# Two low-rank projections of layer 0 moved in beside the modulation, by quarters of their rows

## Chip, core and metric

The kernel runs on one core of a Trainium2 chip. The metric is the device time of one execution in microseconds; lower is better.

## What is computed

Two layers of a trunk in which four token mixers run in parallel on one normalised, modulated input. Layer 0 works on 256 latent and 256 context tokens of 2048 channels:

```python
mod_x = silu(c) @ w_mod[l] + b_mod[l]        # and the same from c_ctx for the context
shift, scale, gate = split(mod_x, 3)
hx = rmsnorm(x, pre_g[l]) * (1 + scale) + shift
px = split_proj(hx @ w_in[l])                # kv 320, cq 512, zA, uB, ... 512 each, gates 8192 columns
q  = rmsnorm(px.cq, q_norm_g) @ w_uq         # low rank, then 4 heads
kv = rmsnorm(px.ckv, kv_norm_g) @ w_ukv
ya = attention(q, kv) * silu(px.zA)
yb = fourier_mix(px.uB) * silu(px.zB)        # yc, yd: a short convolution and a spatial gate
out = (sum over g of sigmoid(gate_g) * (y_g @ w_branch[g])) @ w_out
x  = x + gate * rmsnorm(out, post_g)
```

All of it is in float32.

## The kernel before

Every large product is made from float32 operands that are split into a high and a low half. A chunk of weights is 256 rows by 512 columns (512 KB, one transfer into a `raw` tile of five); ScalarE casts its two halves of 128 rows to `wh` (L236), VectorE subtracts to get `wl` (L239), and TensorE makes three matmuls for each of four output tiles and each 128 rows: high times high, low times high, high times low (L263 to L265 where the features are the rows of the result, L267 to L269 where the tokens are). A projection from 2048 channels is eight such chunks, 192 matmuls into four banks of `acc`; `acc` has five banks, `mis` (transposes, scores) three.

Layer 0 has to make its own modulation first. `mod_products(l, part, j)` makes one part (scale, part 1, or shift, part 0) of 512 columns: eight transfers of 512 KB from `w_mod`, each followed by two narrow matmuls (L315) against the silu of `c` and `c_ctx`, 32 columns wide and in one of four quarters of the array; then a copy on ScalarE (L318), four transposes (L321), and small steps on VectorE (L323, L324, L299, L301). With both parts of a unit of four blocks of 128 channels there, `to_modulate` makes the eight pieces of the input for these channels: ScalarE applies scale and shift (L392), VectorE splits (L208, L209). The rows of `x` and `ctx` are read in four tiles of 1 MB, normalised (L378 on ScalarE, the chain to L387 on VectorE) and transposed (L398) beside the first unit.

The modulation stage runs over four units of four blocks. cq of layer 0 is accumulated in four banks from the first unit to the last: after the first part of unit j, the two chunks of cq for the channels of unit j-1 follow (`first_steps`), and the last two after the stage. Then kv (eight chunks of 320 columns) with the norm of cq beside it, the query and key products with the norm of kv beside them, then zA and uB with the attention of the layer beside both, and the gates.

Work that is to lie beside a projection stands in two queues: `near`, which moves one step at every chunk (`tick`), and `far`, the modulation of later parts on VectorE (`mod_sums`, L338), which moves 0.65 steps a chunk. The framework orders the instructions of each engine at build time from the order of the code; each engine works its list in order and waits on semaphores.

Of the kernel before, what the change touches and what calls it, by code (L numbers as in the profile page):

```python
# [25 lines left out]
P = 128  # L26
# [3 lines left out]
W = 512  # L30
# [6 lines left out]
FIRST_AT = (0, 7)  # L37
# [8 lines left out]
def in_groups():  # L46

    out = {n: (OFF[n], 320 if n == "kv" else W) for n in ORDER}
    for g in range(4):
        for d in range(4):  # L50
            out[f"g{g}{d}"] = (GATES + g * D + d * W, W)
    return out
# [18 lines left out]
def layouts(inp):  # L71
# [6 lines left out]
    for l in range(L):  # L78
        a[f"wi{l}"] = chunked(inp["w_in"][l], gin)
        a[f"wm{l}"] = chunked(inp["w_mod"][l], [slice(i * W, (i + 1) * W) for i in range(12)])  # L80
# [64 lines left out]
def backbone(ctx: ExitStack, tc: tile.TileContext, a, out):  # L145
# [82 lines left out]
    def chunk(src, off, n, on_act=True):  # L228
# [3 lines left out]
        for k in range(KC):  # L232
            h = pw.tile([P, W], F32R, tag="wh", name="wh", bufs=NH)[:, :n]
            l = pw.tile([P, W], F32R, tag="wl", name="wl", bufs=NL)[:, :n]
            if on_act:
                nc.scalar.copy(h, raw[:, k, :])  # L236
            else:
                ve.tensor_copy(h, raw[:, k, :])
# [11 lines left out]
    def projecting(banks, src, off, nk, n, mode, ah, al, on_act=True):  # L250
# [4 lines left out]
        for kc in range(nk // KC):  # L255
            wh, wl = chunk(src, off + kc * KC * P * n, n, on_act)
            for j, kk in order(len(banks), kc == nk // KC - 1):
# [14 lines left out]
    def project(src, off, nk, n, mode, ah, al, size):  # L272

        banks = [bank([P, size]) for _ in range(n // P)] if mode == "f" else [bank([P, n]) for _ in range(size)]
        for _ in projecting(banks, src, off, nk, n, mode, ah, al):
            tick()
        return banks
# [14 lines left out]
    def mod_done(l, part, j, streams, vals):  # L292

        c = slice(j * 4, (j + 1) * 4)
# [10 lines left out]
    def mod_products(l, part, j):  # L305


        b = bank([P, W])
        i = part * 4 + j
        for kc in range(KD // KC):  # L310
            raw = raw_chunk(a[f"wm{l}"], (i * (KD // KC) + kc) * KC * P * W)
            for kk in range(KC):
                k = kc * KC + kk
                q = (k % 4) * 32
                mm(b[q:q + 32, :], cvz[:, k, :], raw[:, kk, :], start=k < 4, stop=k >= KD - 4, tile_position=(0, q))  # L315
            yield
        r = small([P, W])
        nc.scalar.copy(r, b)  # L318
        tr = bank2([P, 4, P])
        for q in range(4):  # L320
            nc.tensor.transpose(tr[:, q, :], r[:, q * P:(q + 1) * P], ident)  # L321
        c2 = pv.tile([P, 4, 2], F32, tag="c2", name="c2", bufs=2)
        ve.reduce_sum(c2, tr.rearrange("p b (q m) -> p b m q", q=4)[:, :, 0:2, :], axis=AX.X)  # L323
        mod_done(l, part, j, (0, 1), lambda v, m: ve.tensor_copy(m, c2[:, :, v]))  # L324

    def mod_sums(l, part, j, streams):
# [27 lines left out]
        mod_done(l, part, j, streams, lambda v, m: ve.reduce_sum(m, own[:, v], axis=AX.X))  # L354
# [51 lines left out]
    first_mod = mod_products(0, 1, 0)  # L406
    for _ in range(3):
        next(first_mod)

# [8 lines left out]
    xs = [big("m", [P, 4, 512]) for _ in range(4)]  # L418

    def rows_in():  # L420
        for v, src in enumerate((a["x"], a["ctx"])):
            tiles = []
            for i in range(2):
                x = big("y" if v + i == 2 else "t", [P, D])
                nc.sync.dma_start(x, src[i * P:(i + 1) * P, :])
                scaled_rows(x)
                tiles.append(x)
                yield
# [36 lines left out]

    h0 = Input(0)
    rows = rows_in()
    cq0 = [bank([P, W]) for _ in range(4)]
    first = projecting(cq0, a["wi0"], offs["cq"], KD, W, "t", *h0.acts("t", W))

    def first_steps(j):
        for _ in range(2):
            next(first)

    def to_modulate(j):
        for k in range(4 * j, 4 * j + 4):
            for v in range(2):
                c = slice(v * NS, (v + 1) * NS)
                modulated(0, k, v, xs[j][:, k % 4, c], [h0.part(k, i, v * NS, (v + 1) * NS) for i in range(2)])
                yield  # L480

    pending = iter(())
    for j in range(4):
        for part in (1, 0):
            g = mod_products(0, part, j) if (part, j) != (1, 0) else first_mod
            for n, _ in enumerate(g):
                if j == 0:
                    next(rows, None)
                next(pending, None)
                if j and (part, n) == FIRST_AT:  # L490
# [5 lines left out]
        pending = to_modulate(j)  # L496
# [4 lines left out]
    first_steps(3)  # L501
# [5 lines left out]
    def layer(l, hx, cq):  # L507
# [7 lines left out]
        def hin(name, mode, tiles=nt):  # L515
            n = 320 if name == "kv" else W
            return project(a[f"wi{l}"], offs[name], KD, n, mode, *hx.acts(mode, T), T if mode == "f" else tiles)
# [8 lines left out]
        def low_rank(bs, n, sizes):  # L526

            raw = big("t", [P, 4, 512])
            ssq = tiny(4)
            for i, b in enumerate(bs):  # L530
                nc.scalar.copy(raw[:, i, :sizes], b[:, :sizes])
                sum_squares(ssq[:, i:i + 1], raw[:, i, :n])
            return raw, ssq, len(bs), n
# [28 lines left out]
        if cq is None:  # L562
            cq = hin("cq", "t")
        cq = low_rank(cq, W, W)
        near.append(normed(cq, qg, qh, ql))
# [3 lines left out]
        kv = hin("kv", "t", 4)  # L569
        drain(near)  # L570
        kv = low_rank(kv, 256, 320)
        raw = kv[0]
        kvs = big("m", [P, 4, 512], F32R)
        kh, kl = kvs[:, 0:2, :], kvs[:, 2:4, :]
        if not last:
            qn = big("t", [P, 4, 512])
        near.append(normed(kv, kg, kh, kl))
# [534 lines left out]
```

## Time and profile before

| | us |
|---|---|
| median of 3 runs | 2648.08 (2646.14 to 2648.66) |
| profiled execution | 2649.58 |
| its span, first to last instruction | 2647.8 |
| TensorE busy | 2597.5 |
| VectorE busy | 1568.4 |
| ScalarE busy | 1032.4 |

The profiled execution is a little longer than its span, since something lies around the first and last instruction. Busy times are those of the engines by themselves; they overlap. A busy TensorE can still run below its full clock, which the granted clock of a stretch tells.

### The profile page before, as it was taken

The page shows a single profiled execution, that of the slowest core. Times are in us where ns is not written, and L with a number is a line of the kernel's source. Part 1 is how long each engine was busy: PE and PEld are TensorE (multiplying, and loading weights), DVE is VectorE, ACT ScalarE, POOL GpSimd, SP SyncE. Part 2 cuts the span into 40 slices and gives each one's busy share as a digit, 9 for nine tenths or more (in the row PEclk, how much of TensorE's full clock was granted, in tenths as well). Part 3 has the DMA queues.
Part 4 walks back from the last instruction along what each step waited for, and adds up shares of the span by engine and source line. Part 5 has one row for each costly group of instructions (what it writes and reads, how often), then busy time and mean ns, then how long its engine had stood idle before and what let it go on. Part 6 is the DMA issues. An engine that isn't in the chain of part 4 may idle for free.

```text
span 2647.8 us, 32990 instructions
## 1 busy us (share of the span) xinstructions
PE 2597.5 (98%) x11739; PEld 2098.5 (79%) x11739; DVE 1568.4 (59%) x2964; ACT 1032.4 (39%) x1881; POOL 11.5 (0%) x25
## 2 busy tenths in 40 slices
PE   6899999999999999999999999999999999999998
PEld 2387788888888888888888888889788888888886
DVE  4277465666666567555563336776555555656666
ACT  3244333222222222222222235565655444545555
POOL 0000000000000000000000000000000000000000
PEclk8999999999999999999999999999999999999999
DMA  8754243444435444445453326754445555566566
GB/s 324 289 181 144 88 135 132 148 159 151 151 136 167 153 151 155 153 141 178 144 177 102 97 97 213 254 167 141 139 151 175 191 193 195 186 208 200 187 219 206
DMA packets 125493, 448.61 MB, mean 169 GB/s; under 512 B 14112, under 2 KB 19408, under 8 KB 123408
## 3 DMA queue, kind: packets, MB, share of 16 engines
q1 hardware_dynamic: 123088, 433.11, 48.6%
q0 software_dynamic: 2240, 13.40, 1.4%
q8 instruction: 92, 1.51, 0.2%
q14 instruction: 73, 0.60, 0.1%
HBM read 442.23 MB, written 4.22 MB: 169 GB/s over the span
## 4 chain that ended last, share of the span: by engine, by line
PE 95%; DMA 2%; DVE 2%; ACT 0%; issue 0%; SPq 0%; DVEq 0%; ACTq 0%
PE acc L263 16%; PE acc L265 16%; PE acc L264 16%; PE acc L269 14%; PE acc L267 14%; PE acc L268 14%; DMA raw<-in_wm 2%; PE acc L315 1%; PE mis L398 1%; PE mis L660 1%; PE mis L661 1%; DVE m L1020 0%; DVE wl L239 0%; PE mis L644 0%; PE mis L857 0%
## 5 line engine op out<-in xcount | busy, mean ns | idle before, releaser
L239 DVE TENSOR_TENSOR wl<-raw,wh 128x512 fp32r<-128x512 f32 (+1 forms) x1256 | 848.0, 682 | 741.0 <-PE acc L265 345.4
L236 ACT CAST wh<-raw 128x512 fp32r<-128x512 f32 (+1 forms) x1256 | 769.6, 617 | 1323.9 <-PE acc L264 814.6
L267 PE MATMUL acc<-wh,hh 128*128 128x512 f32 (+1 forms) x1568 | 611.5, 390 | 0.0
L263 PE MATMUL acc<-hh,wh 128*128 128x512 f32 x1536 | 602.9, 393 | 0.2 <-DVE m L780 0.2
L269 PE MATMUL acc<-wl,hh 128*128 128x512 f32 (+1 forms) x1568 | 601.4, 384 | 1.4 <-DVE wl L239 1.3
L268 PE MATMUL acc<-wh,hl 128*128 128x512 f32 (+1 forms) x1568 | 601.3, 383 | 0.0
L265 PE MATMUL acc<-hh,wl 128*128 128x512 f32 x1536 | 598.3, 390 | 0.0
L264 PE MATMUL acc<-hl,wh 128*128 128x512 f32 x1536 | 598.0, 389 | 0.0
L338 DVE SCALAR_TENSOR_TENSOR ma<-raw,cv,ma 128x512 f32<-128x512 f32 x420 | 298.6, 747 | 141.3 <-DMA raw<-in_wm 139.8
L269 PEld LDWEIGHTS acc<-wl,hh 128*128 128x128 f32 x1568 | 294.3, 188 | 61.5 <-DVE wl L239 4.7
L267 PEld LDWEIGHTS acc<-wh,hh 128*128 128x128 f32 x1568 | 294.8, 188 | 58.2 <-issue 2.9
L268 PEld LDWEIGHTS acc<-wh,hl 128*128 128x128 f32 x1568 | 294.9, 188 | 57.9 <-issue 2.9
L263 PEld LDWEIGHTS acc<-hh,wh 128*128 128x128 f32 x1536 | 288.4, 188 | 61.1 <-DVE m L780 0.8
L265 PEld LDWEIGHTS acc<-hh,wl 128*128 128x128 f32 x1536 | 288.3, 188 | 60.5
L264 PEld LDWEIGHTS acc<-hl,wh 128*128 128x128 f32 x1536 | 288.4, 188 | 60.0 <-issue 0.7
L263 PE MATMUL acc<-y,wh 128*128 128x512 f32 x256 | 101.4, 396 | 0.0
L264 PE MATMUL acc<-y,wh 128*128 128x512 f32 x256 | 100.9, 394 | 0.0
L265 PE MATMUL acc<-y,wl 128*128 128x512 f32 x256 | 100.9, 394 | 0.0
L315 PE MATMUL acc<-raw,g 128*32 128x512 f32 x256 | 64.5, 707 | 24.6 <-DMA raw<-in_wm 24.6
L315 PEld LDWEIGHTS acc<-raw,g 128*32 128x32 f32 x256 | 9.9, 117 | 65.6 <-DMA raw<-in_wm 50.5
L265 PEld LDWEIGHTS acc<-y,wl 128*128 128x128 f32 x256 | 47.9, 187 | 11.8
L263 PEld LDWEIGHTS acc<-y,wh 128*128 128x128 f32 x256 | 47.9, 187 | 11.7
(220 smaller groups left out, 1497.6 us busy)
## 6 DMA issues: line engine op xcount, KB each, us to landing
raw<-in_wi SPq DMA_DIRECT2D x432, 512.0 KB, 3.5
raw<-in_wm SPq DMA_DIRECT2D x192, 512.0 KB, 4.3
raw<-in_wo SPq DMA_DIRECT2D x104, 512.0 KB, 4.2
raw<-in_wb SPq DMA_DIRECT2D x64, 512.0 KB, 4.1
raw<-in_wi SPq DMA_DIRECT2D x16, 320.0 KB, 3.3
t<-row POOLq DMA_DIRECT2D x3, 1024.0 KB, 6.8
t<-in_x SPq DMA_DIRECT2D x2, 1024.0 KB, 9.7
raw<-in_wq SPq DMA_DIRECT2D x4, 512.0 KB, 4.3
```

Of the source, the lines that this page charges most:

```text
L236: nc.scalar.copy(h, raw[:, k, :])
L239: ve.tensor_tensor(l, raw[:, k, :], h.bitcast(F32), ALU.subtract)
L263: mm(b, wh[kk][:, c], xh, start=first, stop=False)
L264: mm(b, wh[kk][:, c], xl, start=False, stop=False)
L265: mm(b, wl[kk][:, c], xh, start=False, stop=last)
L267: mm(b, xh, wh[kk], start=first, stop=False)
L268: mm(b, xl, wh[kk], start=False, stop=False)
L269: mm(b, xh, wl[kk], start=False, stop=last)
L315: mm(b[q:q + 32, :], cvz[:, k, :], raw[:, kk, :], start=k < 4, stop=k >= KD - 4, tile_position=(0, q))
L338: ve.scalar_tensor_tensor(s, raw[:, kk, :], cv[:, k, v:v + 1], s, ALU.mult, ALU.add)
L398: nc.tensor.transpose(dst[:, i * P:(i + 1) * P], x[:, k * P:(k + 1) * P], ident)
L660: mm(s, qn[:, h, c], kn[:, h, k0:512], start=True, stop=False)
```

## The change

Five edits, all in layer 0.

1. The row tiles of `x` and `ctx` are issued to the queue before any weight of the modulation.
2. The modulation's units are now (first block, blocks) = (0,2), (2,2), (4,4), (8,4), (12,4): the first unit of four is cut in two. A unit of four reads alternately a 1 MB tile (in `y`) and two 512 KB tiles, four matmuls to a step.
3. cq and kv are made by quarters of their rows (four blocks of 128 channels): a quarter accumulates in four banks, and its sums go to SBUF (`parked`), copied by ScalarE for the first quarter and added by VectorE for the others. Sixteen pieces of one chunk each, in the order cq, cq, kv, kv for each quarter; `BESIDE` places 0, 1, 3, 4, 3 of them in the five units, the other five come after the last.
4. uB follows kv directly, with the norms of cq and kv as its `near` work.
5. zA has the attention beside it alone, with a `near` step after every half chunk (`fine`).

```diff
-FIRST_AT = (0, 7)
+UNITS = ((0, 2), (2, 2), (4, 4), (8, 4), (12, 4))
...
-    def tick():
+    def tick(whole=True):
         step(near)
-        pace[1] += pace[0]
+        pace[1] += pace[0] if whole else 0.0
...
-    def projecting(banks, src, off, nk, n, mode, ah, al, on_act=True):
+    def projecting(banks, src, off, nk, n, mode, ah, al, fine=False):
...
+            for at, (j, kk) in enumerate(order(len(banks), kc == nk // KC - 1)):
+                if fine and at == len(banks):
+                    yield
...
+    def mod_products(l, part, k0, nk):
+        n = nk * P
+        b = bank([P, n])
+        for s in range(KD // 4):
+            off = moff[l][part * D + k0 * P] + s * 4 * P * n
+            if n < W:
+                raw = pw.tile([P, KC, W], F32, tag="raw", name="raw", bufs=NR).rearrange("p k n -> p (k n)")
+            elif s % 2 == 0:
+                raw = big("y", [P, 2048])
+            else:
+                raw = None
...
+            for i in range(4):
+                mm(b[i * 32:(i + 1) * 32, :], cvz[:, s * 4 + i, :], rows[i], start=s == 0, stop=s == KD // 4 - 1,
+                   tile_position=(0, i * 32))
+            yield
...
+    for v, src in enumerate((a["x"], a["ctx"])):
+        for i in range(2):
+            rows_of[v, i] = x = big("y" if v + i == 2 else "t", [P, D])
+            nc.sync.dma_start(x, src[i * P:(i + 1) * P, :])
...
+    def quarter(name, j):
+        n = 320 if name == "kv" else W
+        if j == 0:
+            parked[name] = big("t", [P, 4, W])
+        banks = [bank([P, n]) for _ in range(4)]
+        ah, al = h0.acts("t", W)
+        for kc in (2 * j, 2 * j + 1):
+            wh, wl = chunk(a["wi0"], offs[name] + kc * KC * P * n, n)
+            for i, kk in order(4, kc % 2):
+                k = kc * KC + kk
+                mm(banks[i], ah(k, i), wh[kk], start=k == 4 * j, stop=False)
+                mm(banks[i], al(k, i), wh[kk], start=False, stop=False)
+                mm(banks[i], ah(k, i), wl[kk], start=False, stop=k == 4 * j + 3)
+            if kc % 2:
+                for i, b in enumerate(banks):
+                    s = parked[name][:, i, :n]
+                    if j == 0:
+                        nc.scalar.copy(s, b)
+                    else:
+                        ve.tensor_tensor(s, s, b, ALU.add)
+            yield
...
+    products = in_turn(*[quarter(name, j) for j in range(4) for name in ("cq", "kv")])
+    BESIDE = (0, 1, 3, 4, 3)
     pending = iter(())
+    for u, (k0, nk) in enumerate(UNITS):
+        at = [1 + 7 * i // max(BESIDE[u], 1) for i in range(BESIDE[u])]
+        for n, _ in enumerate(in_turn(mod_products(0, 1, k0, nk), mod_products(0, 0, k0, nk))):
...
+            if n in at:
+                if n == at[0]:
                     for _ in pending:
                         pass
-                    first_steps(j - 1)
+                next(products)
...
+        pending = to_modulate(k0, nk)
...
-    first_steps(3)
+    for _ in products:
+        pass
...
+        near.append(normed(kv, kg, kh, kl))
         if not last:
+            u = big("t", [P, 4, 512])
+            fourier_in()
+            drain(near)
             qn = big("t", [P, 4, 512])
...
-            za = silu("zA")
-            u = big("t", [P, 4, 512])
-            fourier_in()
+            za = silu("zA", fine=True)
             drain(near)
```

Lines move: the narrow matmul L315 is L337 in the changed file, its copy and transposes L341 and L344, the cast `wh` L245, the modulation L392 is L415, the wide matmuls of cq and kv are L502 to L504.

The queue's list (SP) at the start of the program, before the change; `t` and `y` hold rows, `raw` weights:

```order
3 L225 DMA raw<-in_wm 128x1024 x3
4 L412 DMA cst<-in_const 128x260
5 L225 DMA raw<-in_wm 128x1024
6 L425 DMA t<-in_x 128x2048
7 L225 DMA raw<-in_wm 128x1024
8 L425 DMA t<-in_x 128x2048
9 L225 DMA raw<-in_wm 128x1024 x5
10 L425 DMA t<-in_ctx 128x2048
11 L225 DMA raw<-in_wm 128x1024
12 L425 DMA y<-in_ctx 128x2048
```

and of the changed kernel:

```order
3 L431 DMA cst<-in_const 128x260
4 L442 DMA t<-in_x 128x2048 x2
5 L442 DMA t<-in_ctx 128x2048
6 L442 DMA y<-in_ctx 128x2048
7 L330 DMA raw<-in_wm 128x2x512 x10
8 L235 DMA raw<-in_wi 128x1024
```

Four transfers of weights stood ahead of the first row tile, and eleven ahead of the last; now none does.

ScalarE's list before, from the second unit to the third; L392 is the modulation of the input, L236 the casts of cq's weights:

```order
15 L392 ACTIVATE s<-m,mod_78 128x256 x8
16 L318 COPY s<-acc 128x512 x2
17 L236 CAST wh<-raw 128x512 x2
18 L392 ACTIVATE s<-m,mod_78 128x256 x2
19 L236 CAST wh<-raw 128x512 x2
20 L392 ACTIVATE s<-m,mod_78 128x256 x6
21 L318 COPY s<-acc 128x512 x2
```

and of the changed kernel, from the third unit to the fifth (L415 modulates, L245 casts):

```order
26 L341 COPY s<-acc 128x512
27 L415 ACTIVATE s<-m,mod_78 128x256 x8
28 L245 CAST wh<-raw 128x512 x4
29 L245 CAST wh<-raw 128x320 x2
30 L341 COPY s<-acc 128x512
31 L245 CAST wh<-raw 128x320 x2
32 L341 COPY s<-acc 128x512
33 L415 ACTIVATE s<-m,mod_78 128x256 x8
34 L245 CAST wh<-raw 128x512 x4
```

The casts stood ahead of the pieces of modulation of their own unit; they now stand behind all eight of them.

TensorE's list before, around the first piece of cq:

```order
46 L315 MATMUL acc<-raw,g 32x512 x12
47 L321 MATMUL mis<-cst,s 128x128 x4
48 L315 MATMUL acc<-raw,g 32x512 x16
49 L321 MATMUL mis<-cst,s 128x128 x4
50 L267 MATMUL acc<-wh,hh 128x512
51 L268 MATMUL acc<-wh,hl 128x512
```

and of the changed kernel at the end of the third unit, where the second quarter of cq begins:

```order
149 L337 MATMUL acc<-y,g 32x512 x4
150 L337 MATMUL acc<-raw,g 32x512 x4
151 L344 MATMUL mis<-cst,s 128x128 x4
152 L337 MATMUL acc<-y,g 32x512 x4
153 L337 MATMUL acc<-raw,g 32x512 x4
154 L502 MATMUL acc<-wh,hh 128x512
155 L503 MATMUL acc<-wh,hl 128x512
```

Between the last transposes of a unit and the first product that needs it there stood a whole part (16 narrow matmuls and its transposes); there now stand eight narrow matmuls.

## Rows read from the trace of the kernel before

**Rows 1.** the page: busy time, share of the span and instructions of each engine

```profile
PE 2597.5 (98%) x11739; PEld 2098.5 (79%) x11739; DVE 1568.4 (59%) x2964; ACT 1032.4 (39%) x1881; POOL 11.5 (0%) x25
```

**Rows 2.** waits of PE in the whole span: total us, times, longest

```profile
PE acc L315 <- DMA raw<-in_wm: 24.6, 27, 5.8
PE mis L398 <- DVE t L387: 6.2, 2, 5.1
```

**Rows 3.** stretches: length, PE, PEld, DVE, ACT, POOL busy, granted clock, DMA, GB/s

```profile
0.00:69.17 69.17, 47.56 (x209) 13.96 (x209) 29.79 (x123) 24.08 (x64) 0.20 (x4) 0.90 0.86 327
...
80.87:102.18 21.31, 14.61 (x74) 3.07 (x73) 0.83 (x7) 1.74 (x4) 0.00 (x0) 1.00 0.91 342
...
113.88:138.38 24.50, 17.34 (x74) 4.08 (x73) 0.83 (x7) 2.00 (x4) 0.00 (x0) 0.77 0.83 312
...
10.00:20.00 10.00, 5.33 (x17) 0.96 (x15) 4.32 (x21) 5.12 (x16) 0.00 (x0) 0.71 1.02 413
```

**Rows 4.** PE in order of time, modulation: start, us, operation, idle before

```profile
80.87 2.77 PE L315 MATMUL acc<-raw,g 128*32 128x512 f32 x20
85.53 1.05 PE L315 MATMUL acc<-raw,g 128*32 128x512 f32 x4 [1.89 <-DMA raw<-in_wm]
```

**Rows 5.** PE in order of time, the cq and kv products

```profile
71.24 0.39 PE L267 MATMUL acc<-wh,hh 128*128 128x512 f32 x1
...
80.55 0.39 PE L269 MATMUL acc<-wl,hh 128*128 128x512 f32 x1
...
161.32 0.30 PE L267 MATMUL acc<-wh,hh 128*128 128x320 f32 x1
...
168.21 0.31 PE L269 MATMUL acc<-wl,hh 128*128 128x320 f32 x1
...
191.37 0.31 PE L268 MATMUL acc<-wh,hl 128*128 128x320 f32 x1
```

**Rows 6.** ACT, then DVE in order of time: the four row tiles

```profile
12.42 0.63 ACT L378 ACTIVATE s<-t 128x512 f32<-128x512 f32 x1 [9.74 <-DMA t<-in_x]
...
15.01 0.16 DVE L385 TENSOR_REDUCE n<-n 128x1 f32<-128x4 f32 x1 [11.89 <-ACT s L378]
...
22.34 1.29 DVE L387 TENSOR_SCALAR t<-t,n 128x2048 f32<-128x2048 f32 x1
...
39.80 1.29 DVE L387 TENSOR_SCALAR y<-y,n 128x2048 f32<-128x2048 f32 x1
...
49.38 0.42 DVE L436 COPY m<-mis 128x256 f32<-128x256 f32 x1 [1.15 <-PE mis L398]
```

**Rows 7.** PE, ACT, DVE in order of time: a unit's end and its modulation

```profile
68.65 0.66 PE L321 MATMUL mis<-cst,s 128*128 128x128 f32 x4 [0.73 <-ACT s L318]
...
49.59 0.66 PE L321 MATMUL mis<-cst,s 128*128 128x128 f32 x4
...
50.97 4.04 ACT L392 ACTIVATE s<-m,mod 128x256 f32<-128x256 f32 x8 [1.00 <-DVE mod L299]
...
55.49 0.75 DVE L209 TENSOR_TENSOR hl<-s,hh 128x256 fp32r<-128x256 f32 x2
```

**Rows 8.** stretches of 2 us; columns as in rows 3

```profile
32.00:34.00 2.00, 0.00 (x0) 0.00 (x0) 1.25 (x8) 2.00 (x7) 0.00 (x0) 1.00 0.94 309
34.00:36.00 2.00, 0.00 (x0) 0.00 (x0) 1.72 (x9) 0.89 (x4) 0.00 (x0) 0.69 0.90 334
...
40.00:42.00 2.00, 2.00 (x6) 0.56 (x5) 1.31 (x2) 0.12 (x1) 0.00 (x0) 0.60 0.64 190
42.00:44.00 2.00, 1.97 (x10) 0.86 (x9) 0.95 (x3) 0.85 (x3) 0.00 (x0) 1.00 0.87 344
```

**Rows 9.** groups by shape to 420 us: busy, mean ns, idle before, releaser

```profile
L338 DVE SCALAR_TENSOR_TENSOR ma<-raw,cv,ma 128x512 f32<-128x512 f32 x93 | 66.3, 745 | 22.4 <-DMA raw<-in_wm 22.4
L663 DVE TENSOR_REDUCE n<-mis 128x1 f32<-128x512 f32 x8 | 5.5, 690 | 7.6 <-PE mis L661 7.5
...
L666 ACT ACTIVATE s<-mis,n 128x512 f32<-128x512 f32 x8 | 5.5, 689 | 16.9 <-DVE n L664 16.9
```

More of the change, by code (lines that the diff above doesn't have):

```diff
@@ L51, in in_groups, with mod_groups @@
             out[f"g{g}{d}"] = (GATES + g * D + d * W, W)
+    return out
+def mod_groups(l):
+    out = []
+    for part in range(3):
+        units = UNITS if l == 0 and part < 2 else [(4 * j, 4) for j in range(4)]
+        out += [(part * D + k * P, n * P) for k, n in units]
     return out
@@ L303, in mod_done @@
                 ve.tensor_tensor(m, m, vecs[l][:, 86:102][:, c], ALU.mult)
[L305 to L315, printed above, removed]
+    moff = {l: {c: D * c for c, _ in mod_groups(l)} for l in range(L)}
@@ L466, in backbone @@
     h0 = Input(0)
[L467 to L476, printed above, removed]
+    parked = {"cq": None, "kv": None}
+    def quarter(name, j):
[16 more added lines that the diff above has]
+                        nc.scalar.copy(s, b)
+                    else:
+                        ve.tensor_tensor(s, s, b, ALU.add)
+            yield
@@ L477, in to_modulate, with in_turn @@
+    def to_modulate(k0, nk):
+        for k in range(k0, k0 + nk):
             for v in range(2):
                 c = slice(v * NS, (v + 1) * NS)
-                modulated(0, k, v, xs[j][:, k % 4, c], [h0.part(k, i, v * NS, (v + 1) * NS) for i in range(2)])
+                modulated(0, k, v, xs[k // 4][:, k % 4, c], [h0.part(k, i, v * NS, (v + 1) * NS) for i in range(2)])
                 yield
-    pending = iter(())
[L483 to L487, printed above, removed]
+    def in_turn(*gens):
+        for g in gens:
+            yield from g
@@ L523, in cols, with low_rank @@
             return lambda k, j: h[:, k, j * P:(j + 1) * P], lambda k, j: l_[:, k, j * P:(j + 1) * P]
-        def low_rank(bs, n, sizes):
-            raw = big("t", [P, 4, 512])
+        def low_rank(name, n, sizes, tiles):
             ssq = tiny(4)
-            for i, b in enumerate(bs):
-                nc.scalar.copy(raw[:, i, :sizes], b[:, :sizes])
+            if last:
+                bs = hin(name, "t", tiles)
+                raw = big("t", [P, 4, 512])
+            else:
+                raw = parked[name]
+            for i in range(tiles):
+                if last:
+                    nc.scalar.copy(raw[:, i, :sizes], bs[i][:, :sizes])
                 sum_squares(ssq[:, i:i + 1], raw[:, i, :n])
-            return raw, ssq, len(bs), n
+            return raw, ssq, tiles, n
         def normed(rows, g, dh, dl):
@@ L568, in layer @@
             drain(near)
-        kv = hin("kv", "t", 4)
-        drain(near)
-        kv = low_rank(kv, 256, 320)
+        kv = low_rank("kv", 256, 320, 4)
+        if last:
+            drain(near)
         raw = kv[0]
@@ L683, in silu @@
                 yh, yl = halves()
-            for f, b in enumerate(hin(name, "f")):
+            for f, b in enumerate(hin(name, "f", fine=fine)):
                 s = small([P, 512])[:, :T]
```

81 lines of the change are left out of this document (39 added, 42 removed).

## The prediction

> **What bounds the kernel now.** I read the page first: TensorE is busy for 98% of the span [rows 1], so a change can win only where TensorE waits, runs slowly, or does a thing twice. Then the waits of TensorE: nearly all of the idle time stands at two places, in front of the modulation's products (for weights) and in front of the transposes of the input rows (for VectorE) [rows 2]. Both lie in the first 138 us. The stretches of that stage [rows 3] show the pattern: between two pieces of cq, 21.3 and 24.5 us in which TensorE is busy for 14.6 and 17.3 us, while the transfers run at 342 and 312 GB/s. After that stage TensorE works without a gap, kv included. So what the change is worth is read from the start of the program to the end of kv, at 191.5 us (the last start of [rows 5] and the 0.15 us that one takes); what follows (the query and key products, attention, zA, uB) is the same TensorE work in both kernels, 44 us of uB included, which only changes places with kv.
>
> The reference point is therefore this: before, cq and kv are done at 191.5 us. In the changed kernel the same state is the start of uB. The four groups of transposes of cq's norm, 0.45 us each (0.66 with the drain of the last in it [rows 7]), stand ahead of that point before and behind it now, 1.8 us. The gain is 191.5 - 1.8 - X, where X is the time at which uB starts.
>
> **What the change adds up to, step by step.**
>
> *The input rows.* All four row tiles are now issued ahead of any weight, after 0.2 MB of constants. Before, the first tile was there at 12.4 us [rows 6], behind some 2 MB of weights and shared with more of them; at 413 GB/s [rows 3] those 2 MB are 5 us, so I take 8 us (bounds 6.5 and 10). ScalarE's sums take 2.6 us (12.42 to 15.01), then VectorE needs 8.6 us for two tiles (15.01 to 22.34 + 1.29), 4.3 each and 17.2 for four; on it also lie eight copies of the first half, 0.42 us each, 3.4. The second half's transposes and copies took from 41.1 to 49.8 us, 8.7 [rows 6]. That is 8 + 2.6 + 17.2 + 3.4 + 8.7 = 39.9, where the trace of before has 49.8. The modulation of the first two blocks of 128 columns lies beside this; its end needs 2.6 us (small copies, one cast of 0.6, one subtraction of 0.7, a first modulated piece). The first product starts at **42.5 us** (bounds 40, and 52.4 if the rows come no sooner).
>
> *The products.* cq is 192 matmuls: 42 of them from 71.24 to 80.55, 0.227 us apart; kv is 192, 48 from 161.32 to 168.21, 0.147 apart [rows 5]. 43.6 + 28.2 = **71.8 us**, unchanged in number.
>
> *The modulation's products.* One transfer of 512 KB gives two matmuls, each recorded twice: 20 records in 2.77 us are five transfers, 0.55 us each when the weights are there; a lone one takes 1.05 [rows 4]. Of the 64, ten lie in the first 42.5 us, 54 x 0.55 = 29.7, and seven groups of four transposes, 3.1: **32.8 us**. That the weights are there: by the end of the last unit the queue has moved 42.7 MB (64 x 0.524, 4.2 of rows, six cq and five kv chunks); at the 327 GB/s of the first stretch [rows 3] that is 131 us, and my sum has that end at 143. The 1 MB tiles help here, but transfers are not the term that sets X.
>
> *The new wait, at the hand-over of a unit.* Before, cq's piece j came a whole part (eight transfers) after the modulation of its rows; the cast of its weights stood ahead of the pieces of modulation on ScalarE. Now the product of a unit stands three steps behind the end of that unit, and the order of ScalarE shows eight pieces of modulation, and only then the casts that the product waits for. Price [rows 7]: 0.73 us copy, 1.38 from the transposes to the first piece (49.59 to 50.97), 4.04 for the eight, 0.62 for a cast: 6.8, with latencies 6.9 us. VectorE ends its last split at 56.24 and then has a subtraction of 0.7, 7.3 us after the transposes began, which the first four matmuls cover. Meanwhile TensorE has its transposes (0.45) and four transfers' products (2.2): 4.25 us are left, at two hand-overs (k 4 to 7, k 8 to 11). The unit of two blocks has half the pieces, 2.3. After the last unit nothing is left to fill with: kv's third quarter is ready in its data, but its casts stand behind the same eight pieces, 6.45. Sum **17.3 us**. If the pieces hid as before, 0; if VectorE ends it instead of ScalarE, 2 us more.
>
> *The clock.* [...] Four hand-overs with idle stretches of 2.3 to 6.4 us: **8.6 us** (bounds 0, and 22 from the rival below). [...]
>
> *Smaller ones.* Sums now leave the banks after each quarter: seven of eight quarters end in four VectorE adds or ScalarE copies beside the next piece; I take 0.3 us for each of ten starts of a piece, **3.0** (bounds 0 and 6).
>
> X = 42.5 + 71.8 + 32.8 + 17.3 + 8.6 + 3.0 = 176.0, and the gain 191.5 - 1.8 - 176.0 = 13.7 us.
>
> *uB beside the norms* costs nothing: the norms' 24 transposes wait on VectorE while uB's 192 matmuls, 44 us, run; uB itself needs only the modulated input. If that cover failed, it is the one wait of 1.1 us that cq's norm has before.
>
> *zA beside attention.* The 16 steps of attention now stand 12 matmuls (2.7 us) apart instead of 24. A step's chain is maximum 0.69, exponential 0.69 [rows 9], some 0.5 of small ones: 1.9 us, and the far queue's four accumulations of 0.745 can stand ahead on VectorE, 3.0: 4.9. A score bank comes round after 2.7 plus 0.5 to 2 us of attention's own matmuls. I take 0; worst 1.5 us at five steps, 7.5.
>
> The profiled execution took 2649.6 us around its span of 2647.8; less 13.7 it is 2635.9. The median of the runs shown is 1.5 us lower, so I forecast **2634 us**.
>
> **The rivals.**
> *A. The clock holds, and the rows come early.* For it: the stretch 80.87 to 102.18 is idle for a third and yet at full clock [rows 3]. Against: the clock at 34 to 42 us [rows 8]. The gain is 13.7 + 8.6 + 2.5 = 24.8: 2623 us.
> [...]
> *C. Slower: attention becomes the bound.* Place: the score matmuls, waiting for a bank that the exponential of the step before still reads. It decides from 13.7 / 16 = 0.86 us a step; with 1.5 at every step it is 24 us, 10 slower: 2658. For it: the 4.9 against 3.2 to 4.7 above. Against: the far queue only moves at every second tick, at 0.65 a tick, and the mean load of VectorE per step is about 3 of 5 us.
> *D. The rows come no sooner*, since ScalarE or the queue sets them: X + 9.9, gain 4, 2644.
>
> **How the numbers follow.** The forecast, with a gain of 6 to 20: 0.52. A: 0.25, with an open end to some 32 us. B: 0.10. D: 0.08. C: 0.05. The range reaches over the forecast, most of A and most of D: 2619 to 2645; its own part alone is 2628 to 2642. A measurement of this kernel tells about 0.2%, 5.3 us, from no change: faster is the forecast, A, and a little of D, 0.80; same is B and most of D, 0.15; slower is C, 0.05.
>
> **What would show it.** Right: the first wide matmul of cq at 40 to 45 us; at four places behind it TensorE idle for 2 to 7 us, released by ScalarE's casts or VectorE's halves, not by a transfer, each followed by some 4 us at a granted clock of 0.5; uB's first matmul at 170 to 182; no wait of the score matmuls. The waits for weights fall from 24.6 to under 8 us. Wrong: waits for weights that remain above 15 us (then transfers, and the 2 KB runs of the narrow units, set X), the clock at 1.00 through all hand-overs (A), or idle time at the scores (C).

## The result: slower, and where the time went

The changed kernel took 2666.33 us (median of 4 runs, 2665.01 to 2668.45) against 2648.37 us of the kernel before in the same runs, a ratio of 1.0067 with a 95% interval of 1.005 to 1.0085: slower by 0.7%. The forecast was 2634 us. The profiled execution of the changed kernel took 2668.45 us around a span of 2666.6.

The page of the changed kernel, busy time of each engine; TensorE is as full as in [rows 1], with 16 us more of it:

```profile
PE 2613.7 (98%) x11803; PEld 2103.3 (79%) x11803; DVE 1583.2 (59%) x3000; ACT 1028.6 (39%) x1881; POOL 11.7 (0%) x25
```

The waits of TensorE in the changed kernel (total us, times, longest):

```profile
PE mis L421 <- DVE t L410: 17.9, 2, 14.6
PE acc L502 <- ACT wh L245: 7.3, 3, 5.2
PE acc L502 <- DVE hh L218: 4.5, 2, 3.4
PE mis L344 <- ACT s L341: 3.4, 5, 0.8
PE acc L337 <- DMA raw<-in_wm: 2.6, 3, 2.2
PE mis L421 <- DVE y L410: 2.0, 1, 2.0
PE acc L278 <- DVE wl L246: 1.0, 3, 0.5
PE acc L337 <- DMA y<-in_wm: 0.6, 1, 0.6
```

The 24.6 us of waits for the modulation's weights [rows 2] have become 3.2 (2.6 and 0.6). In their place stand 7.3 us for ScalarE's casts `wh` and 4.5 for VectorE's halves `hh`, the hand-overs of the prediction (1.13 of the 4.5 are ahead of the first product of cq). The waits ahead of the transposes of the input rows grew from 6.2 us [rows 2] to 19.9 (17.9 for `t`, 2.0 for `y`); they lie ahead of the first product. No score matmul waits. The same stage in order of time, on TensorE (start, us, operation, idle before it):

```profile
41.53 0.74 PE L502 MATMUL acc<-wh,hh 128*128 128x512 f32 x2 [1.13 <-DVE hh L218]
...
57.84 0.50 PE L502 MATMUL acc<-wh,hh 128*128 128x512 f32 x1 [1.06 <-ACT wh L245]
...
84.09 0.50 PE L502 MATMUL acc<-wh,hh 128*128 128x512 f32 x1 [1.09 <-ACT wh L245]
...
117.34 0.79 PE L502 MATMUL acc<-wh,hh 128*128 128x512 f32 x1 [3.41 <-DVE hh L218]
...
147.97 0.64 PE L502 MATMUL acc<-wh,hh 128*128 128x320 f32 x1 [5.17 <-ACT wh L245]
...
172.56 0.39 PE L276 MATMUL acc<-wh,hh 128*128 128x512 f32 x1
```

The first product of cq is at 41.5 us and uB's first product at 172.56. By the prediction's reference point the gain there is 191.5 - 1.8 - 172.56 = 17.1 us, more than the 13.7 forecast. So the changed kernel loses behind this point what it won and 19 us more (2668.45 against 2649.58 us, the profiled executions). Behind it TensorE hardly waits at all: from 600 to 2600 us it is busy for 1998.9 of the 2000 us. What differs is the beat of the wide products, the time from the start of one to the start of the next. TensorE in order of time at 600 us, first the changed kernel, then the kernel before:

```profile
600.05 0.39 PE L274 MATMUL acc<-hh,wl 128*128 128x512 f32 x1
600.28 0.40 PE L272 MATMUL acc<-hh,wh 128*128 128x512 f32 x1
600.52 0.39 PE L273 MATMUL acc<-hl,wh 128*128 128x512 f32 x1
600.75 0.40 PE L274 MATMUL acc<-hh,wl 128*128 128x512 f32 x1
600.98 0.39 PE L272 MATMUL acc<-hh,wh 128*128 128x512 f32 x1
601.21 0.40 PE L273 MATMUL acc<-hl,wh 128*128 128x512 f32 x1
```

```profile
599.91 0.39 PE L263 MATMUL acc<-hh,wh 128*128 128x512 f32 x1
600.13 0.39 PE L264 MATMUL acc<-hl,wh 128*128 128x512 f32 x1
600.36 0.39 PE L265 MATMUL acc<-hh,wl 128*128 128x512 f32 x1
600.59 0.39 PE L263 MATMUL acc<-hh,wh 128*128 128x512 f32 x1
600.81 0.39 PE L264 MATMUL acc<-hl,wh 128*128 128x512 f32 x1
601.04 0.39 PE L265 MATMUL acc<-hh,wl 128*128 128x512 f32 x1
```

Five steps take 1.16 us in the one and 1.13 in the other, with no idle time noted between them and the same operations. The groups by shape show it as a mean duration that is a little longer (busy us, mean ns), from 172 us on in the changed kernel and from 191 us on in the kernel before:

```profile
L272 PE MATMUL acc<-hh,wh 128*128 128x512 f32 x1536 | 614.7, 400 | 0.6 <-DVE m L837 0.6
...
L276 PE MATMUL acc<-wh,hh 128*128 128x512 f32 x1376 | 546.0, 397 | 0.0
```

```profile
L263 PE MATMUL acc<-hh,wh 128*128 128x512 f32 x1536 | 602.9, 393 | 0.2 <-DVE m L780 0.2
...
L267 PE MATMUL acc<-wh,hh 128*128 128x512 f32 x1376 | 545.4, 396 | 0.0
```

A matmul's end is modelled in the profile (records of 0.39 us start 0.23 us apart above), so the distance of starts is the better measure. Over all wide products behind 191.5 us it is, on average, 226.9 ns before and 233.3 after in the form that streams `hh` or `hl` against weights `wh` or `wl` (layer 0, 3 x 1536 products), and 227.2 against 229.0 in the form that streams `wh` or `wl` against `hh` or `hl` (mainly layer 1, 3 x 1376). That is 4608 x 6.4 ns + 4128 x 1.8 ns = 36.9 us. With the 17.1 won, 2649.6 - 17.1 + 36.9 = 2669.4 us, and the profiled execution took 2668.45: the account closes within 1 us.

Why should the same products stand further apart? The diff holds one thing that acts on all of them: the row tiles `t` and `y` are allocated ahead of `h0 = Input(0)`, which allocates `hh` and `hl`. In both built programs these tags lie in the order in which they are first asked for. The start of each tag in a partition of SBUF, in bytes, from the two:

```
        wh     wl     m       hh      hl      t       y
before  46816  59104  85728   118496  151264  184032  208800
after   46816  59104  85728   159648  192416  118496  143264
```

Modulo 256, `wh`, `wl` and `m` are at 224 in both; `hh` and `hl` are at 224 before and at 160 after; `y` is at 160 in both. This was the theory to test ("place"), against the rival that the new order of work (half-chunk steps of zA, uB's new place, the later far queue) makes the products stand apart ("order").

### The profile page after: what moved, and what is told of

Same layout as the page of the kernel before. It is cut to its first block, busy times and chain, and to the rows that moved or that the text cites. A ratio compares the mean times of both kernels' runs of the same rounds, so it can differ in the third digit from the quotient of the medians.

```text
span 2666.6 us, 33124 instructions
## 1 busy us (share of the span) xinstructions
PE 2613.7 (98%) x11803; PEld 2103.3 (79%) x11803; DVE 1583.2 (59%) x3000; ACT 1028.6 (39%) x1881; POOL 11.7 (0%) x25
## 4 chain that ended last, share of the span: by engine, by line
PE 96%; DVE 2%; issue 1%; DMA 1%; ACT 0%; SPq 0%; DVEq 0%; ACTq 0%
PE acc L272 16%; PE acc L273 16%; PE acc L274 16%; PE acc L278 13%; PE acc L276 13%; PE acc L277 13%; PE acc L502 1%; PE acc L504 1%; PE acc L503 1%; PE acc L337 1%; PE mis L421 1%; PE mis L717 1%; PE mis L718 1%; DVE m L1075 0%; DMA raw<-in_wm 0%
## 5 line engine op out<-in xcount | busy, mean ns | idle before, releaser
L245 ACT CAST wh<-raw 128x512 fp32r<-128x512 f32 (+1 forms) x1256 | 767.7, 615 | 1359.7 <-PE acc L273 818.0
L272 PE MATMUL acc<-hh,wh 128*128 128x512 f32 x1536 | 614.7, 400 | 0.6 <-DVE m L837 0.6
L273 PE MATMUL acc<-hl,wh 128*128 128x512 f32 x1536 | 607.4, 395 | 0.0
L274 PE MATMUL acc<-hh,wl 128*128 128x512 f32 x1536 | 607.2, 395 | 0.0
L278 PE MATMUL acc<-wl,hh 128*128 128x512 f32 (+1 forms) x1440 | 559.6, 389 | 1.1 <-DVE wl L246 1.0
L277 PE MATMUL acc<-wh,hl 128*128 128x512 f32 (+1 forms) x1440 | 558.6, 388 | 0.0
L272 PEld LDWEIGHTS acc<-hh,wh 128*128 128x128 f32 x1536 | 288.7, 188 | 72.1 <-issue 1.9
L274 PEld LDWEIGHTS acc<-hh,wl 128*128 128x128 f32 x1536 | 288.6, 188 | 69.6
L278 PEld LDWEIGHTS acc<-wl,hh 128*128 128x128 f32 x1440 | 270.5, 188 | 60.1 <-DVE wl L246 3.5
L277 PEld LDWEIGHTS acc<-wh,hl 128*128 128x128 f32 x1440 | 270.7, 188 | 56.8 <-issue 1.9
L276 PEld LDWEIGHTS acc<-wh,hh 128*128 128x128 f32 x1440 | 270.6, 188 | 56.0 <-issue 1.9
L272 PE MATMUL acc<-y,wh 128*128 128x512 f32 x256 | 101.7, 397 | 0.0
L274 PE MATMUL acc<-y,wl 128*128 128x512 f32 x256 | 101.2, 395 | 0.0
L502 PE MATMUL acc<-wh,hh 128*128 128x512 f32 (+1 forms) x128 | 48.4, 381 | 11.9 <-ACT wh L245 7.3
L274 PEld LDWEIGHTS acc<-y,wl 128*128 128x128 f32 x256 | 48.1, 188 | 11.6
L272 PEld LDWEIGHTS acc<-y,wh 128*128 128x128 f32 x256 | 48.1, 188 | 11.5
L273 PEld LDWEIGHTS acc<-y,wh 128*128 128x128 f32 x256 | 48.1, 188 | 11.5
```

The lines of the kernel that those rows point to most:

```text
L272: mm(b, wh[kk][:, c], xh, start=first, stop=False)
L273: mm(b, wh[kk][:, c], xl, start=False, stop=False)
L274: mm(b, wl[kk][:, c], xh, start=False, stop=last)
L276: mm(b, xh, wh[kk], start=first, stop=False)
L277: mm(b, xl, wh[kk], start=False, stop=False)
L278: mm(b, xh, wl[kk], start=False, stop=last)
```

## The experiments

All diffs are against the changed kernel unless another one is named (in 9 to 11 it is the kernel of experiment 5). Intervals are of the ratio to the kernel before in the same runs. Experiments 1 to 4, 5 to 8 and 9 to 12 ran on three chips, where the kernel before took 2648.78, 2648.78 and 2647.7 us; so about 1 us between an experiment of 9 to 12 and one of 5 to 8 means nothing.

**1. The old places under the new order.**

```diff
     xs = [big("m", [P, 4, 512]) for _ in range(4)]
+    h0_tiles = [wide() for _ in range(KD)]
     rows_of = {}
...
-            self.t = [wide() for _ in range(KD)]
+            self.t = h0_tiles if l == 0 else [wide() for _ in range(KD)]
```

> The changed kernel with one thing put back: the 32 tiles hh and hl are allocated ahead of the row tiles t and y, so that hh, hl, t and y lie at the same SBUF addresses as in the kernel before. The instructions and their order on every engine are those of the changed kernel. Theory 'place': the loss comes from where the operands of the wide products lie in SBUF, so the wide products stand about 227 ns apart again, uB still begins at about 172 us, and the time is that of before less some 17.5 us: 2631 us (2627 to 2635). Rival 'order': the loss comes from the new order of the work (half-chunk steps of zA beside attention, uB beside the norms, later far work); the spacing stays at 233 ns from 300 to 1600 us and the time at 2666 us.

Measured: 2632.97 us (0.994, 0.9926 to 0.9955), 227 ns. The loss is gone with the places alone; the order of work does not cause it.

**2. The new places under the old order**, against the kernel before.

```diff
-                x = big("y" if v + i == 2 else "t", [P, D])
+                x = row_tiles[v, i]
...
+    row_tiles = {(v, i): big("y" if v + i == 2 else "t", [P, D]) for v in range(2) for i in range(2)}
     h0 = Input(0)
```

> The kernel before with one thing changed: the four row tiles (t and y) are allocated ahead of hh and hl, so that hh, hl, t and y lie at the SBUF addresses of the changed kernel. Instructions and order are those of the kernel before. Theory 'place': the wide products of layer 0 stand 233 ns apart, those of layer 1 229 ns, and the time rises by what the changed kernel lost behind 172 us, some 36 us: 2684 us (2675 to 2690). Rival 'order': 2648 us, 227 ns.

Measured: 2682.75 us (1.0131, 1.0114 to 1.0148), with 233.3 and 229.1 ns. TensorE in order of time at 600 us in this run; the five steps take 1.16 us, as in the changed kernel:

```profile
599.98 0.39 PE L265 MATMUL acc<-hh,wl 128*128 128x512 f32 x1
600.21 0.40 PE L263 MATMUL acc<-hh,wh 128*128 128x512 f32 x1
600.45 0.39 PE L264 MATMUL acc<-hl,wh 128*128 128x512 f32 x1
600.68 0.40 PE L265 MATMUL acc<-hh,wl 128*128 128x512 f32 x1
600.91 0.39 PE L263 MATMUL acc<-hh,wh 128*128 128x512 f32 x1
601.14 0.40 PE L264 MATMUL acc<-hl,wh 128*128 128x512 f32 x1
```

**3 and 4. Region or offset: 64 bytes left free ahead of `hh`**, once in the changed kernel, once in the kernel before, by the same line.

```diff
+    pb.tile([P, 16], F32, tag="pad", name="pad", bufs=1)
     h0 = Input(0)
```

> The changed kernel with 64 bytes left free ahead of hh, so that hh and hl lie 64 bytes higher (offset 96 in 128 bytes, as wh, wl and m and as in the kernel before, where the changed kernel has 32), in the same upper region of SBUF. If the offset within 128 bytes is what counts: 2631 us, 227 ns. If the region, or the distance of hh and hl from wh, counts: 2666 us, 233 ns. Rival 'order': 2666 us.

> The kernel before with 64 bytes left free ahead of hh, so that hh, hl, t and y lie 64 bytes higher (hh and hl at offset 32 in 128 bytes, as in the changed kernel, where the kernel before has 96), in the same lower region. If the offset within 128 bytes counts: about 2684 us and 233 ns. If the region or the distance counts: 2648 us, 227 ns. Rival 'order': 2648 us.

Measured: 2631.53 us (0.9935, 0.992 to 0.9949) and 2676.61 us (1.0104, 1.0089 to 1.0119). One line that computes nothing takes 35 us from the one kernel and adds 28 to the other. So it is the offset, and not the region. TensorE at 600 us in the changed kernel with 64 bytes free, 1.14 us for five steps:

```profile
599.79 0.39 PE L272 MATMUL acc<-hh,wh 128*128 128x512 f32 x1
600.02 0.39 PE L273 MATMUL acc<-hl,wh 128*128 128x512 f32 x1
600.25 0.39 PE L274 MATMUL acc<-hh,wl 128*128 128x512 f32 x1
600.47 0.39 PE L272 MATMUL acc<-hh,wh 128*128 128x512 f32 x1
600.70 0.39 PE L273 MATMUL acc<-hl,wh 128*128 128x512 f32 x1
600.93 0.39 PE L274 MATMUL acc<-hh,wl 128*128 128x512 f32 x1
```

The expectation of 2684 us for the fourth run was 7 too high, and the two forms changed roles: 229.0 ns where `hh` or `hl` is streamed, 233.3 where they are the weights. So an offset of 32 (229.0 ns where `h` is streamed) is not what an offset of 160 is (233.3 in the changed kernel), though both are 32 modulo 128: the period is not 128 bytes. 256 fits: `hh` starts 71680 bytes behind `wh` in the kernel before (280 x 256) and 112896 behind it in experiment 3 (441 x 256), at 226.9 and 227.0 ns.

**5. All operands at one offset:** the 64 bytes between `t` and `y`, which moves `y`, `hh` and `hl` to 224.

```diff
         for i in range(2):
+            if v + i == 2:
+                pb.tile([P, 16], F32, tag="pad", name="pad", bufs=1)
             rows_of[v, i] = x = big("y" if v + i == 2 else "t", [P, D])
```

> The changed kernel with 64 bytes left free between t and y instead of ahead of hh: now y, hh and hl all start at the offset of wh, wl and m (224 in 256 bytes); up to here y stood 64 below it in every fast kernel, and the products of y were 233.3 ns apart in the feature-major form (768 of them) and 229 in the row-major form (384). Theory 'difference of offsets': all wide products 227 ns, 768 x 6.3 + 384 x 2 = 5.6 us less than the 2631.5 us of the run with 64 bytes ahead of hh: 2626 us. Rival 'only hh and hl count, or the region': 2631.5 us and y's products as before.

Measured: 2625.4 us (0.9911, 0.9895 to 0.9928). The products of `y`, slow in the kernel before as well, went to 226.8 ns.

**6. Own offset or difference:** the places of the first experiment, and 64 bytes ahead of `wh`.

```diff
         raw = raw_chunk(src, off, n)
+        if not unused:
+            unused.append(pw.tile([P, 16], F32, tag="pad", name="pad", bufs=1))
         wh, wl = [], []
```

> The changed kernel with the old order of places (hh and hl ahead of t and y), and 64 bytes left free ahead of wh in the pool of weights, so that wh, wl, m, hh and hl all lie 64 bytes higher (offset 32 in 256 bytes for all of them); their differences are those of the run with the old places. Theory 'difference of offsets': 227 ns and 2633 us as there. Rival 'each tile's own offset': with hh at 32 the feature-major products were 229 ns and the row-major 233.3, with the weights at 224; if own offsets count, wh at 32 adds to that, at least 4608 x 2 + 4300 x 6.3 = 36 us: 2669 us or more.

Measured: 2631.75 us (0.9935, 0.992 to 0.9949), 227.0 ns with `wh`, `wl`, `hh` and `hl` all at 32. Moving both operands of a product by 64 bytes changed nothing (227.0 ns in experiment 1 too); moving one of them against the other did (226.9 ns before, 229.0 in experiment 4).

**7 and 8. Other differences.** The second has 32 and 8 in place of 8 and 16. `Input(0)` takes these tiles as in experiment 1, and both runs give up four small vectors (`bufs=12` for `n`) for the room.

```diff
+    h0_tiles = [[None, None] for _ in range(KD)]
+    for i, (tag, free) in enumerate((("hh", 8), ("hl", 16))):
+        pb.tile([P, free], F32, tag="pad" + tag, name="pad" + tag, bufs=1)
+        for k in range(KD):
+            h0_tiles[k][i] = pb.tile([P, W], F32R, tag=tag, name=tag, bufs=KD)
```

> The changed kernel with hh 32 bytes and hl 96 bytes above the offset of the weights (modulo 256) and y 32 above, to read other differences than 0, +64 and -64 (four of the sixteen small vectors of the norms are given up for the room). No theory has a value for them; if the spacing goes with the difference, each form of product has one spacing for each difference, between 226 and 236 ns, and a product of hl another than one of hh. In the row-major form the weights of the array are hh or hl and the stream is wh; if it is the tile being streamed against the weights that are loaded next, the spacing goes with the following product's tile. Time between 2626 (all as at 0) and 2670 us.

> As the run before, with hh 128 bytes and hl 160 bytes above the offset of the weights (modulo 256) and y 96 above. If only the offset within 128 bytes counted, hh would read as at difference 0, 227 ns; if the period is 256 bytes, it may be anything from 226 to 240. Time between 2626 and 2700 us.

Measured: 2675.86 us (2 runs), 6 us above the range that was expected, and 2666.12 us (2 runs). The expectation that a product goes by its own tile alone fell: in the seventh run the two products that stream `hh` (L272 and L274) stand 234.9 and 230.5 ns ahead of the next one. A difference of 128 cannot be read from the eighth, since `hh` at 128 and `hl` at 160 follow each other: of its streaming products the one between two streams of `hh` (L274 to L272) has 226.1 ns, the two beside `hl` have 230.9 and 230.0.

The mean distance of starts in all these runs, behind 191.5 us, worked out from the starts in each trace (all neighbours 200 to 260 ns apart: some 4500, 3900, 760 and 381 in the four columns). "Differs" is the start of the tile less that of `wh`, modulo 256; the four columns on the right are ns, for the products in which `h` (`hh` or `hl`) or `y` is streamed and those in which it is the weights. Experiments 9 to 11 read as 5 does.

```
run                       h differs  y differs  stream h  weights h  stream y  weights y
before                        0        192        226.9     227.2      233.3     229.0
changed                     192        192        233.3     229.0      233.4     228.9
1 old places                  0        192        227.0     227.2      233.3     229.0
2 before, new places        192        192        233.3     229.1      233.3     228.9
3 changed, 64 free            0        192        227.0     227.2      233.3     229.0
4 before, 64 free            64          0        229.0     233.3      227.5     227.8
5 all equal                   0          0        226.9     227.1      226.8     226.8
6 weights moved too           0        192        227.0     227.1      233.3     229.0
7                         32, 96        32        232.3     232.2      233.4     233.3
8                       128, 160        96        229.0     233.3      233.6     234.4
12 before, all equal          0          0        226.9     227.1      226.8     226.8
```

The table reads the same for `h` and for `y`: stream less weights = 0 gives 226.8 to 227.8 ns, 192 gives 233.3, 64 gives 229. In the form where the tile is the weights the sign turns, and so do the two numbers. These are means. At 0 and at 192 the three products of a triple agree within 0.5 ns (226.7, 227.0 and 227.1 before; 233.3 three times in the changed kernel); at 64 they need not: in experiment 4, with every `h` at 64, they stand 230.9 (L263), 226.9 (L264) and 229.2 ns (L265) ahead of the next. So the difference modulo 256 does not settle every beat by itself.

**9. zA's half-chunk steps**, on the run with all offsets equal.

```diff
-            za = silu("zA", fine=True)
+            za = silu("zA")
```

> The run with all offsets equal (2625.4 us), with zA's steps beside attention as before, one for each whole chunk instead of two. The prediction put the half-chunk steps at 0 (worst 7.5 us). If they cost nothing: 2625 us (2621 to 2629). If the score matmuls wait for a bank because steps come too close together: down to 2618. If the half steps are worth something (attention ends earlier, less is drained without cover): up to 2632.

Measured: 2625.67 us (0.9916, 0.9903 to 0.993). The steps cost and bring nothing that can be told from the noise.

**10. uB back behind zA**, on the run with all offsets equal.

```diff
             fourier_in()
-            drain(near)
+        drain(near)
...
-            u = big("t", [P, 4, 512])
-            fourier_in()
-            drain(near)
             qn = big("t", [P, 4, 512])
...
             za = silu("zA", fine=True)
+            u = big("t", [P, 4, 512])
+            fourier_in()
             drain(near)
```

> The run with all offsets equal (2625.4 us), with uB's products put back behind zA, as in the kernel before, so that the norms of cq and kv are drained with nothing beside them. The prediction put uB's new place at 0 and the loss of its cover at the 1.1 us of cq's norm. With cq and kv both waiting for their norm's first step on VectorE (row norms, about 3 to 5 us each, as no product stands beside them): 2630 us (2626 to 2636). If uB's place costs something that the trace hides: below 2624.

Measured: 2631.97 us (0.9938, 0.9926 to 0.9951), 6.6 above the run with all offsets equal. Two of its waits on TensorE that run 5 does not have, in front of the norms' transposes and of the key's (total us, times, longest):

```profile
PE mis L604 <- DVE t L599: 3.1, 1, 3.1
...
PE mis L657 <- DVE s L645: 0.9, 1, 0.9
```

A wait of 0.5 us for ScalarE follows the first of them. Behind that idle time the granted clock falls: 0.86 from 172 to 176 us and 0.71 from 176 to 180, where run 5 has 1.00 in both; the missing shares are 1.7 us at most, as TensorE is idle for a part of it. So the waits (4.5 us) and the clock make up about 6 of the 6.6 us.

**11. The casts ahead of the modulation pieces**, on the run with all offsets equal.

```diff
+    def cast_ahead():
+        name, kc = steps.pop(0)
+        n = 320 if name == "kv" else W
+        cast.append(chunk(a["wi0"], offs[name] + kc * KC * P * n, n))
...
-            wh, wl = chunk(a["wi0"], offs[name] + kc * KC * P * n, n)
+            if not cast:
+                cast_ahead()
+            wh, wl = cast.pop(0)
...
+        cast_ahead()
         pending = to_modulate(k0, nk)
```

> The run with all offsets equal (2625.4 us), with the weights of the first cq or kv piece behind each unit cast ahead of that unit's modulation pieces instead of behind them on ScalarE. There TensorE waited 8.2 us for ScalarE's casts and 4.5 us for VectorE's halves at the hand-overs (1.65, 3.42 and 5.17 the longest), and the granted clock was 0.93, 0.78 and 0.91 in the three stretches behind, about 5 us lost. Theory of the prediction, the wait is the queue on ScalarE: the casts fit into the 1.4 us that ScalarE waits for the modulation vector, the product starts with the first piece's halves, about 4 us sooner; waits fall to 2 us or less, and some clock comes back: 2614 us (2610 to 2618). Rival, VectorE ends the wait: its subtraction of the weights (1.28 us) now stands ahead of the halves; 2625 us or up to 3 us more.

Measured: 2619.8 us (0.9894, 0.9881 to 0.9908), the fastest kernel here. The waits at the hand-overs, with the one ahead of the first product, fell from 12.7 to 3.4 us (total us, times, longest):

```profile
PE acc L514 <- ACT wh L245: 2.0, 2, 1.7
...
PE acc L514 <- DVE hh L218: 1.4, 2, 0.7
```

The granted clock stayed at its upper level in the stretches behind the hand-overs. Three stretches, first of the changed kernel, then of this run (length; PE, PEld, DVE, ACT, POOL busy; granted clock; transfers, GB/s). The run with all offsets equal has a granted clock of 0.93, 0.78 and 0.91 in them.

```profile
118.00:142.00 24.00, 23.38 (x124) 15.64 (x122) 7.64 (x19) 3.03 (x6) 0.00 (x0) 0.89 0.71 270
142.00:148.00 6.00, 0.68 (x5) 0.45 (x5) 4.40 (x19) 4.57 (x11) 0.00 (x0) 0.67 0.36 113
148.00:172.00 24.00, 24.00 (x117) 21.77 (x118) 16.89 (x35) 9.78 (x23) 0.00 (x0) 0.87 0.49 154
```

```profile
118.00:142.00 24.00, 21.86 (x131) 14.24 (x130) 7.72 (x24) 3.79 (x9) 0.00 (x0) 1.00 0.85 317
142.00:148.00 6.00, 4.25 (x25) 3.57 (x24) 5.68 (x20) 5.94 (x12) 0.00 (x0) 1.00 0.43 150
148.00:172.00 24.00, 23.71 (x122) 20.51 (x121) 18.77 (x43) 10.83 (x29) 0.00 (x0) 1.00 0.48 161
```

And yet only 5.6 us of the expected 11 came, and the time lies outside the expected 2610 to 2618. uB starts at 164.91 us there, against 170.92. The trace shows two reasons for a part of that. The first two hand-overs behind the first product had waits of 1.35 and 1.65 us in the run with all offsets equal; both are gone, and cq's second quarter still starts at 84.59 us, against 84.24. Ahead of it the modulation's products come by single transfers in both runs: four records take 1.05 us, as long as eight do where the weights are there (1.06), and each transfer is waited for, first in the run with all offsets equal, then in this one:

```profile
80.24 1.05 PE L337 MATMUL acc<-raw,g 128*32 128x512 f32 x4 [0.21 <-DMA raw<-in_wm]
```

```profile
82.34 1.05 PE L337 MATMUL acc<-raw,g 128*32 128x512 f32 x4 [0.22 <-DMA raw<-in_wm]
```

From 41 to 82 us the transfers are busy for 0.96 of the time in both runs. Further, TensorE waits longer for ScalarE's copy ahead of the modulation's transposes, 4.9 us in seven places, against 3.4 in five:

```profile
PE mis L344 <- ACT s L341: 4.9, 7, 0.8
```

That the transfers set the time of the first place is argued from these rows and was not tried, and the rest of the missing 5 us stays open.

**12. The kernel before with all offsets equal**, by the line of experiment 5, against the kernel before.

> The kernel before with 64 bytes left free between t and y, so that y too has the offset of the weights; order of work unchanged. By the difference of offsets: 768 x 6.3 + 384 x 2 ns = 5.6 us less than before: 2643 us (2640 to 2645). Against it, the changed kernel with all offsets equal (2625.4 us) shows the worth of the new order of work alone: 17.4 us, where the prediction had 13.7.

Measured: 2642.05 us (0.9978, 0.9969 to 0.9987). With all offsets equal in both, the new order of work is worth 2642.05 - 2625.4 = 16.7 us (16.4 with experiment 9, which ran on the same chip).

## Why the prediction was wrong, step by step

**The step that failed** is the sentence "what follows (the query and key products, attention, zA, uB) is the same TensorE work in both kernels". It is the same list of instructions, and the prediction took the same list for the same time. The change moved two allocations, those moved the operands of 8736 products, and each then took on average 1.8 or 6.4 ns more: 36.9 us, in no term of the sum. Experiments 1 to 6 show this from both sides. Nothing in the profile of the kernel before warned of it by name, but the trace of that kernel held the effect: its products of `y` stand 233.3 ns apart and its products of `hh` 226.9, the same operation on the same shapes. The question why would have led to the offsets.

**The first product at 42.5 us:** 41.53, right, and by the chain that was told: the first row tile was there at 7.59 us (8 in the sum), the last copy of the second half, ScalarE's, ended at 40.03 (39.9). Rival D is out.

**The hand-overs, 17.3 us:** in kind as told, ScalarE's casts behind eight pieces; in size 13.6. The price of the sum runs from ScalarE's copy on, so the wait for that copy (0.54, 0.78, 0.73 and 0.78 us) belongs to each hand-over beside the wait ahead of the product (1.06, 1.09, 3.41 and 5.17). That makes 1.6, 1.9, 4.1 and 6.0 us, where the sum had 2.3, 4.25, 4.25 and 6.45. Only the second is far off: there TensorE waited for weights instead (0.62, 0.21 and 0.24 us), and the products beside the hand-over took 3.6 us (79.38 to 83.00) and not 2.2. Experiment 11 shows the cause: casts ahead, and the waits ahead of the products go, though not all of the time that they were worth comes back.

**The clock, 8.6 us:** 6.2 measured, and that the two are as near as that is luck. The term was the author's estimate for a loss at each of four hand-overs, and no run shows a loss at four. What the changed kernel showed in its place: the granted clock was 1.00 from 41.5 to 112 us, which takes in the first two, and fell at the other two alone (TensorE at work again at 117.34 and 147.97 us; length, busy times and granted clock as above):

```profile
117.34:123.50 6.16, 6.16 (x15) 4.81 (x16) 3.16 (x6) 1.60 (x3) 0.00 (x0) 0.50 0.86 345
147.97:154.20 6.23, 6.23 (x22) 5.98 (x23) 4.80 (x11) 2.67 (x6) 0.00 (x0) 0.50 0.50 160
```

Half of the two stretches is lost, 6.2 us. The kernel before has one such loss that [rows 8] shows in part. TensorE takes up work again at 36.88 us there, after 5.08 us without it, and the granted clock is 0.50 (columns as above):

```profile
36.00:38.00 2.00, 1.12 (x7) 0.71 (x11) 1.79 (x8) 0.00 (x0) 0.00 (x0) 0.50 0.14 51
38.00:40.00 2.00, 2.00 (x9) 0.35 (x2) 1.65 (x11) 0.00 (x0) 0.00 (x0) 0.50 0.00 0
```

The 0.60 from 40 to 42 us [rows 8] puts the rise from 0.50 to 1.00 at 41.6, 4.7 us after TensorE took up work. Half of that is lost, and four times as much would be 9.4 us. In experiment 11, where no wait for ScalarE's casts or VectorE's halves is longer than 1.7 us, the granted clock is at 1.00 in the three stretches shown. Rival A is out, since the clock fell at two places, and so is B, by which the time would have stayed the same: at uB's start the gain is 17.1 us.

**uB's start at 176.0 us:** 172.56, and a gain of 17.1 instead of 13.7 there. That this is so near is in part luck, since errors cancel: the first product (1.0 us), the hand-overs (3.7) and the clock (2.4) took less than the sum had; against them stand 3.2 us of waits for weights, which the sum put at nothing ("That the weights are there"), and 0.5 for one more copy. The other terms together came out as told. At equal places the whole kernel gains 16.7 (experiments 5 and 12), so the kind of gain in the first stage was told rightly, and it is not given back by any wait behind it.

**uB beside the norms, 0:** right as the change stands, but the price without that cover was put too low, at 1.1 us; experiment 10 measured 6.6. The prediction took the wait of the kernel before for the price; without a projection beside it the norm's wait was 3.1 us and the granted clock behind it was 0.86 and 0.71, in two stretches of 4 us.

**zA beside attention, 0:** right (experiment 9: 0.3 us). Rival C, the slower case, fell although the kernel is slower: no score matmul waits.

## What to carry to other kernels

A moved allocation can change a kernel's time even if no instruction changes (by 34 us in experiment 2): print the addresses of the operands of the main loop ahead of and behind an edit, and measure an edit of the order at equal addresses. In this kernel the wide products stood closest, 226.8 to 227.8 ns apart on average, where their two operands start at the same offset modulo 256 bytes, and 228.9 to 234.4 ns apart at the other differences; the test is one unused tile of 64 bytes. When a page shows a TensorE that never waits and yet is slower, compare the distance of starts of one product, tile by tile: the kernel before, with 226.9 and 233.3 ns for one shape, held its own warning.

## What the hardware showed that was not expected

TensorE's beat for a 128x128 by 128x512 fp32r product depended on where its two operands lie relative to each other: on average 226.9 ns at a difference of 0, 229.0 at +64 (stream less weights, modulo 256), 233.3 at 192, and 232.2 to 234.4 in the runs with 32 and 96, at a granted clock of 1.00. In a kernel with some 10,000 such products that is 1.5% of the time (the kernel before: 2682.75 us in experiment 2 against 2642.05 in experiment 12). In these runs the beat goes with the two starts against each other: with both operands moved by 64 bytes it stayed at 227.0 ns (experiment 6). Whether the weight load or the stream of a product is held up no run here shows; nor why at +64 single products differ by 4 ns (226.9 and 230.9 in experiment 4). A difference of exactly 128 for both halves was not tried.
